# Input projection of a hybrid encoder block: channel groups as one 512-column and one 256-column matmul per weight tile, with the two half sums added after the group

## The chip, the cores and the metric

The kernel runs on one NeuronCore of one Trainium2 chip. The metric is the device time of one execution in microseconds (us); the kernel before takes 1093.23 us, the median of 3 runs (1092.92 to 1093.92). TensorE does the matmuls (PE in the profile, with its weight loads as PEld), VectorE is DVE, ScalarE is ACT, GpSimd is POOL, and SP issues the transfers.

## The reference, cut to what matters

One encoder layer for 256 tokens of width 2048, in float32:

```
h = rmsnorm(x, norm_mix_g)
z = h @ w_in                                   # 2048 x 5120
a, g, q, k, v = split(z)                       # 1024 columns each
u = causal_dwconv(a * sigmoid(g), 31 taps)     # per channel, along tokens
conv_out = silu(layernorm(u))
attn_out = diff_attention(q, k, v)             # 8 heads, rmsnorm per head
x = x + concat(conv_out, attn_out) @ w_out
gate, up = split(rmsnorm(x) @ w_up)            # 2 x 5632 columns
x = x + (gelu(dwconv3(gate)) * up) @ w_down
out = rmsnorm(x)
```

## The kernel before, in words

**Precision by splitting.** A float32 product is made from three matmuls in the type float32r. Every weight chunk is fetched as `raw` (1 MB a transfer, queue of SP), then ACT casts it to `hi` (L156) and DVE computes `lo = raw - hi` (L157), 128 x 1024 elements at a time; the activations stand in `xT` (tile `actT`) as `[P, KD, 2, T]`, high part at index 0 and low part at index 1. A product is hi·high + hi·low + lo·high. The pool of `raw`, `hi` and `lo` has three buffers of each, so ACT and DVE can be at most three chunks ahead of TensorE; a chunk is 4 of the 16 values of k of a group.

**Two ways to build 256 output channels.** `channel_group` (L200) serves the input projection. For each k (16 of them) and each half n of the 256 channels it issues three 256-column matmuls, L206 (hi·high), L207 (hi·low) and L208 (lo·high), all into one accumulator of 128 x 256. `wide_group` (L177) serves the FFN's up projection (44 groups). It issues one 512-column matmul L185 (hi over high and low, which are neighbours in `xT`) into an accumulator of 128 x 2 x 256, and one 256-column matmul L188 (lo over high) into the second half of it. `halves` (L230) then adds the two half sums: ACT copies the second half to a temporary `half` (L232), DVE adds the first half to it (L233).

**Order of the stage.** The first group of a and g channels (j = 0) is built while the input arrives (L260). From then on TensorE's order is written out by hand: for j = 1 to 3 a group of a channels and one of g channels; v columns of heads 0 to 3 (`v_slab`, L216 to L218); then for j = 0 to 3 a group of q and one of k channels, with the remaining v columns after j = 2 and j = 3; then the output projection. That makes 14 groups by `channel_group`. The order on ACT, DVE and SP is chosen by a scheduler that plays the program through with its own cost estimates and priorities; loads are 200 instructions ahead of their place, attention 300.

**What runs beside it.** After every fourth k, `tick` (L166) emits the next background step: attention pieces of the previous head pair (scores L401 and L404, flips L432, values, norm, store L473) and, at two a tick, taps of the 31-tap convolution (L315 to L331; four of six kinds multiply on ACT, L323, and add on DVE, L324; the others are two instructions on DVE, L328). The taps of one channel pair form a chain through its accumulator `cv`. When all are done, `ln_total` (L535) sums the channels on DVE and `ln_mean` (L540) is the matmul that makes the LayerNorm's mean; it has a fixed place in TensorE's order, behind the first two values of k of the output projection.

**What leaves the accumulators before.** For a and g of j = 1 to 3 one DVE multiplication by `rb1` reads the accumulator (L353, L361). For q one ACT copy (L506). For k one DVE multiplication (L511). Each is 128 x 256. The accumulators' pool has four banks, two for each group.

Of the kernel before, what the change touches and what calls it, by code (L numbers as in the profile page):

```python
# [9 lines left out]
F32 = mybir.dt.float32  # L10
F32R = mybir.dt.float32r
AF = mybir.ActivationFunctionType
ALU = mybir.AluOpType
# [3 lines left out]
P = 128  # L17
# [10 lines left out]
def block_kernel(  # L28
# [15 lines left out]
    nc = tc.nc  # L44
    T, D = dims["T"], dims["D"]
    NT = T // P
    KD = D // P
    CONV_K, CC = dims["conv"]
    NCT = CC // P
    H = NCT  # L50
    FK, DFF = dims["ffn"]
    NF = DFF // P
    GW = 2 * P
# [10 lines left out]
    acc = ctx.enter_context(tc.tile_pool(name="acc", bufs=4, space=PSUM))  # L64
# [66 lines left out]
    RATE_A = 2  # L131
    RATE_V = 2
    RATE_Q = 2
# [10 lines left out]
    def load(w, k0, nk, c0, ncol, ahead=None, raw=None):  # L144
        spans = c0 if isinstance(c0, list) else [(c0, ncol)]
        with prio(AHEAD if ahead is None else ahead):
            if raw is None:
                raw = wpool.tile([P, nk, ncol], F32, name="raw")
            fetch(raw, w.tile(k0, nk, spans))
            parts = []  # L150
            hk = min(nk, HALF // ncol)
            for i in range(0, nk, hk):
                hi = wpool.tile([P, hk, ncol], F32R, name="hi")
                lo = wpool.tile([P, hk, ncol], F32R, name="lo")
                src = raw[:, i : i + hk, :]
                nc.scalar.copy(hi, src)  # L156
                nc.vector.tensor_tensor(lo, src, hi.bitcast(F32), op=ALU.subtract)  # L157
                for j in range(hk):
                    parts.append((k0 + i + j, hi[:, j, :], lo[:, j, :]))
        return parts  # L160
# [13 lines left out]
            credit[0] -= 1  # L174
            conv_ops.pop(0)()

    def wide_group(w, c0, xT):  # L177
        ps = [acc.tile([P, 2, T], F32, name="acc") for _ in range(2)]
        for kc in range(0, KD, 8):
            for k, hi, lo in load(w, kc, 8, c0, GW):  # L180
                for n in range(2):
                    cs = slice(n * P, (n + 1) * P)

                    def big(last):
                        nc.tensor.matmul(ps[n], lhsT=hi[:, cs], rhs=xT[:, k], start=(k == 0), stop=last)  # L185

                    def small_(last):
                        nc.tensor.matmul(  # L188
                            ps[n][:, 1, :], lhsT=lo[:, cs], rhs=xT[:, k, 0, :], start=False, stop=last
                        )  # L190

                    if k < KD - 1:
                        big(False)
                        small_(False)
                    else:
                        small_(False)
                        big(True)
        return ps

    def channel_group(w, c0, xT, n_conv=0, ready=None):  # L200
        ps = [acc.tile([P, T], F32, name="acc") for _ in range(2)]
        for kc in range(0, KD, 8):
            for k, hi, lo in ready[kc : kc + 8] if ready else load(w, kc, 8, c0, GW):
                for n in range(2):
                    cs = slice(n * P, (n + 1) * P)
                    nc.tensor.matmul(ps[n], lhsT=hi[:, cs], rhs=xT[:, k, 0, :], start=(k == 0), stop=False)  # L206
                    nc.tensor.matmul(ps[n], lhsT=hi[:, cs], rhs=xT[:, k, 1, :], start=False, stop=False)  # L207
                    nc.tensor.matmul(ps[n], lhsT=lo[:, cs], rhs=xT[:, k, 0, :], start=False, stop=(k == KD - 1))  # L208
                if k % 4 == 3:
                    tick(n_conv)  # L210
        return ps

# [14 lines left out]
    def token_banks(width=XW):  # L227
        return [acc.tile([P, width], F32, name="acc") for _ in range(NT)]

    def halves(dst, ps, pool):  # L230
        t1 = pool.tile([P, T], F32, name="half")
        nc.scalar.copy(t1, ps[:, 1, :])  # L232
        nc.vector.tensor_tensor(dst, ps[:, 0, :], t1, op=ALU.add)  # L233

    with ph1:
        nc.scalar.activation(const.tile([P, 8], F32, name="touch"), mhalf, AF.Copy)
# [3 lines left out]
        xT = shared.tile([P, KD, 2, T], F32R, name="actT")  # L240
        rstd1 = const.tile([P, NT], F32, name="rstd1")
        ss1 = const.tile([P, NT, D // XW], F32, name="ss1")
        rb1 = p1.tile([P, T], F32, name="rb1")
        stage = p1.tile([P, 2, KD * T], F32, name="mixT")
        xraw = stage[:, 0, :].rearrange("p (k t) -> p k t", k=KD)
        wi = w_in
        first = [acc.tile([P, T], F32, name="acc") for _ in range(4)]
# [17 lines left out]
        early = load(wi, 0, 8, GW, GW)  # L265
        for i in range(D // XW):
            if i == 2:
                early.extend(load(wi, 8, 4, GW, GW))
            cs = slice(i * XW, (i + 1) * XW)
# [73 lines left out]
        ordered = ExitStack()  # L343
        ordered.enter_context(tc.manual_schedule(engines={mybir.EngineType.PE}))
        for j in range(NP):
            pa = first[:2] if j == 0 else channel_group(wi, j * GW, xT, n_conv=RATE_A, ready=early if j == 1 else None)
            an, gn = [], []
            for n in range(2):
                a_ = p2.tile([P, T], F32, name=f"a{n}")
                if j == 0:  # L350
                    with prio(ATT):
                        nc.scalar.copy(a_, pa[n])  # L352
                nc.vector.tensor_tensor(a_, a_ if j == 0 else pa[n], rb1, op=ALU.mult)  # L353
                an.append(a_)
            pg = first[2:] if j == 0 else channel_group(wi, CC + j * GW, xT, n_conv=RATE_A)
            for n in range(2):
                g_ = p2.tile([P, T], F32, name="g_")
                if j == 0:
                    with prio(ATT):
                        nc.vector.tensor_copy(g_, pg[n])  # L360
                nc.vector.tensor_tensor(g_, g_ if j == 0 else pg[n], rb1, op=ALU.mult)  # L361
                gn.append(g_)
            for n in range(2):
                c = 2 * j + n
                g_ = gn[n]
                nc.scalar.activation(g_, g_, AF.Sigmoid)
                nc.vector.tensor_tensor(upad[c][:, PADW:], an[n], g_, op=ALU.mult)  # L367
            for k in range(CONV_K):
                conv_ops.append(lambda j=j, k=k: conv_tap(j, k))
# [129 lines left out]

        pending = None  # L500
        for j in range(H // 2):
            pq = channel_group(wi, 2 * CC + j * GW, xT, n_conv=RATE_Q)
            qT, kT = [], []
            for n in range(2):
                q_ = p2.tile([P, T], F32, name=f"q{n}")
                nc.scalar.copy(q_, pq[n])  # L506
                qT.append(q_)
            pk = channel_group(wi, 2 * CC + H * P + j * GW, xT, n_conv=RATE_Q)
            for n in range(2):
                k_ = p2.tile([P, T], F32, name=f"k{n}")  # L510
                nc.vector.tensor_tensor(k_, pk[n], rb1, op=ALU.mult)  # L511
                kT.append(k_)
            a0, a1, a2, a3, a4, a5 = attention(j, qT, kT)
            if j < H // 2 - 1:
                if j < H // 2 - 2:
                    bg.extend([seq(pending, a0), a1, None, None, a2, a3, a4, None])
                else:
                    bg.extend([seq(pending, a0), a1, None, None, None, None, a2, a3, a4])
                pending = a5
            else:  # L520
                last_attention = (a0, a1, a2, a3, a4, a5)
            if j == H // 2 - 2:
                v_slab(H // 2, H // 4)
                bg.extend([None, None, pending])
# [111 lines left out]
    with ExitStack() as ph2:  # L636
# [10 lines left out]
        for j in range(DFF // GW):  # L647
            pg = wide_group(wu, j * GW, h2T)
            ge = []
            for n in range(2):  # L650
                f = 2 * j + n
                gp = gps[f % 4]
                halves(gp[:, FP:], pg[n], q2)
                nc.vector.tensor_tensor(gp[:, FP:], gp[:, FP:], rb2, op=ALU.mult)
                gc = q2.tile([P, T], F32, name=f"gc{n}")
                nc.vector.tensor_scalar(
                    gc, gp[:, 0:T], col["fw"][:, f : f + 1], col["fb"][:, f : f + 1], op0=ALU.mult, op1=ALU.add
                )
                nc.vector.scalar_tensor_tensor(
                    gc, gp[:, 1 : 1 + T], col["fw"][:, NF + f : NF + f + 1], gc, op0=ALU.mult, op1=ALU.add  # L660
                )
                nc.vector.scalar_tensor_tensor(
                    gc, gp[:, 2 : 2 + T], col["fw"][:, 2 * NF + f : 2 * NF + f + 1], gc, op0=ALU.mult, op1=ALU.add
                )
                nc.scalar.activation(gc, gc, AF.Gelu)
                nc.vector.tensor_tensor(gc, gc, rb2, op=ALU.mult)
                ge.append(gc)
            pu = wide_group(wu, DFF + j * GW, h2T)
            for n in range(2):
                f = 2 * j + n  # L670
                us = q2.tile([P, T], F32, name="us")
                halves(us, pu[n], q2)
                nc.vector.tensor_tensor(us, us, ge[n], op=ALU.mult)
                nc.scalar.copy(fT[:, f, 0, :], us)
                nc.vector.tensor_tensor(fT[:, f, 1, :], us, fT[:, f, 0, :].bitcast(F32), op=ALU.subtract)
# [149 lines left out]
```

## Time and profile before

| what | value |
|---|---|
| time, median of 3 runs | 1093.23 us (1092.92 to 1093.92) |
| profiled execution: its time | 1093.6 us |
| profiled execution: first to last instruction (span) | 1091.8 us |
| mean granted TensorE clock | 0.997 of full speed |
| TensorE busy (matmuls) | 1080.2 us, 99% |
| DVE busy | 764.6 us, 70% |
| ACT busy | 599.1 us, 55% |
| L206, L207, L208 (projection groups) | 448 each, 286, 283 and 283 ns mean |
| L185 and L188 (FFN groups) | 1408 each, 395 and 280 ns mean |

The duration of one matmul is longer than the distance from one matmul's start to the next's, because matmuls are pipelined; what a group costs is read from counts in a stretch of time, not from durations. The span and the time differ by 1.8 us that lie before the first and after the last instruction.

### The profile page before, as it was taken

How to read it: one execution, taken by the hardware profiler on the slowest of the kernel's cores; microseconds unless marked ns; L12 is line 12 of the kernel's file. 1: busy time of each engine (PE TensorE's matmuls, PEld its weight loads, DVE VectorE, ACT ScalarE, POOL GpSimd, SP SyncE). 2: the span in 40 equal slices, each digit the busy share in tenths (PEclk: the TensorE clock that was granted, in tenths of full speed). 3: DMA queues.
4: the chain of work that ended last, by engine and by line, in shares of the span. 5: the costliest groups of instructions: out<-in, count | busy, mean ns of one | idle time of the engine just before them, and what ended most of it. 6: DMA issues, size and time to landing. Idle time of an engine off the chain costs nothing.

```text
span 1091.8 us, 16120 instructions
## 1 busy us (share of the span) xinstructions
PE 1080.2 (99%) x6307; PEld 951.6 (87%) x6307; DVE 764.6 (70%) x1201; ACT 599.1 (55%) x974; POOL 16.3 (1%) x44
## 2 busy tenths in 40 slices
PE   9999999999999999999999999999999999999996
PEld 9999999998888888888888888888888888888885
DVE  6799999998665777776777777776777445454544
ACT  6777788886755544544545454444545334343432
POOL 0000000001000000000000000000000000000000
PEclk9999999999999999999999999999999999999998
DMA  9755544453555555555555555555555655555552
GB/s 334 257 185 170 192 164 157 143 189 119 204 179 193 184 182 183 187 189 193 194 193 185 184 183 186 189 193 193 193 189 177 235 196 194 194 195 193 191 176 103
DMA packets 32845, 205.89 MB, mean 189 GB/s; under 512 B 3713, under 2 KB 4481, under 8 KB 9601
## 3 DMA queue, kind: packets, MB, share of 16 engines
q1 hardware_dynamic: 32624, 203.82, 54.0%
q8 instruction: 49, 0.80, 0.3%
q0 software_dynamic: 144, 1.05, 0.2%
q14 instruction: 28, 0.22, 0.1%
HBM read 202.75 MB, written 2.10 MB: 188 GB/s over the span
## 4 chain that ended last, share of the span: by engine, by line
PE 97%; ACT 1%; DVE 1%; DMA 0%; POOL 0%; issue 0%; SPq 0%; POOLq 0%; DVEq 0%; ACTq 0%
PE acc L185 30%; PE acc L188 15%; PE acc L216 11%; PE acc L217 11%; PE acc L218 11%; PE acc L206 5%; PE acc L208 5%; PE acc L207 5%; PE acc L260 2%; PE misc L609 0%; PE misc L404 0%; PE misc L401 0%; DMA v_sb<-in_w_in 0%; PE misc L473 0%; PE misc L432 0%; ACT misc L273 0%
## 5 line engine op out<-in xcount | busy, mean ns | idle before, releaser
L157 DVE TENSOR_TENSOR lo<-raw,hi 128x1024 fp32r<-128x1024 f32 x368 | 449.9, 1223 | 268.9 <-ACT hi L156 268.1
L156 ACT CAST hi<-raw 128x1024 fp32r<-128x1024 f32 x368 | 386.7, 1051 | 392.5 <-PE acc L218 172.7
L185 PE MATMUL acc<-actT,hi 128*128 128x512 f32 x1408 | 481.7, 395 | 0.0
L188 PE MATMUL acc<-actT,lo 128*128 128x256 f32 x1408 | 368.8, 280 | 0.0
L185 PEld LDWEIGHTS acc<-actT,hi 128*128 128x128 f32 x1408 | 253.3, 188 | 48.5
L188 PEld LDWEIGHTS acc<-actT,lo 128*128 128x128 f32 x1408 | 265.4, 188 | 13.7
L217 PE MATMUL acc<-lo,fT 128*128 128x512 f32 (+1 forms) x355 | 137.5, 387 | 0.0
L218 PE MATMUL acc<-hi,fT 128*128 128x512 f32 (+1 forms) x355 | 137.5, 387 | 0.0
L206 PE MATMUL acc<-actT,hi 128*128 128x256 f32 x448 | 128.0, 286 | 0.5 <-ACT a L352 0.5
L208 PE MATMUL acc<-actT,lo 128*128 128x256 f32 x448 | 127.0, 283 | 0.2 <-DVE lo L157 0.2
L207 PE MATMUL acc<-actT,hi 128*128 128x256 f32 x448 | 126.8, 283 | 0.0
L216 PE MATMUL acc<-hi,fT 128*128 128x512 f32 (+1 forms) x355 | 123.8, 387 | 0.0
L206 PEld LDWEIGHTS acc<-actT,hi 128*128 128x128 f32 x448 | 85.9, 192 | 2.0 <-issue 1.0
L208 PEld LDWEIGHTS acc<-actT,lo 128*128 128x128 f32 x448 | 85.9, 192 | 0.4 <-DVE lo L157 0.4
L207 PEld LDWEIGHTS acc<-actT,hi 128*128 128x128 f32 x448 | 85.9, 192 | 0.0
L218 PEld LDWEIGHTS acc<-hi,fT 128*128 128x128 f32 x355 | 66.7, 188 | 13.7
L217 PEld LDWEIGHTS acc<-lo,fT 128*128 128x128 f32 x355 | 66.7, 188 | 13.6
L216 PEld LDWEIGHTS acc<-hi,fT 128*128 128x128 f32 x355 | 66.7, 188 | 13.5
L323 ACT ACTIVATE tap<-u,cols 128x256 f32<-128x256 f32 x160 | 70.7, 503 | 2.7 <-DVE u L367 1.3
L232 ACT COPY half<-acc 128x256 f32<-128x256 f32 x88 | 32.4, 368 | 57.2 <-PE acc L185 57.2
L324 DVE TENSOR_TENSOR cv<-cv,tap 128x512 f32<-128x512 f32 x80 | 54.5, 685 | 1.7
L217 PE MATMUL acc<-lo,mixT 128*128 128x512 f32 x128 | 50.2, 392 | 0.0
(179 smaller groups left out, 914.2 us busy)
## 6 DMA issues: line engine op xcount, KB each, us to landing
raw<-in_w_up SPq DMA_DIRECT2D x88, 1024.0 KB, 4.9
raw<-in_w_down SPq DMA_DIRECT2D x43, 1024.0 KB, 5.0
raw<-in_w_in SPq DMA_DIRECT2D x35, 1024.0 KB, 4.9
raw<-in_w_out SPq DMA_DIRECT2D x14, 1024.0 KB, 4.9
mixT<-in_w_in SPq DMA_DIRECT2D x4, 512.0 KB, 8.6
x_sb<-in_x SPq DMA_DIRECT2D x4, 512.0 KB, 11.1
raw<-in_w_out SPq DMA_DIRECT2D x4, 512.0 KB, 3.5
out<-x_sb SPq DMA_DIRECT2D x8, 256.0 KB, 2.9
```

The source lines that it names most:

```text
L156: nc.scalar.copy(hi, src)
L157: nc.vector.tensor_tensor(lo, src, hi.bitcast(F32), op=ALU.subtract)
L185: nc.tensor.matmul(ps[n], lhsT=hi[:, cs], rhs=xT[:, k], start=(k == 0), stop=last)
L188: nc.tensor.matmul(ps[n][:, 1, :], lhsT=lo[:, cs], rhs=xT[:, k, 0, :], start=False, stop=last)
L206: nc.tensor.matmul(ps[n], lhsT=hi[:, cs], rhs=xT[:, k, 0, :], start=(k == 0), stop=False)
L207: nc.tensor.matmul(ps[n], lhsT=hi[:, cs], rhs=xT[:, k, 1, :], start=False, stop=False)
L208: nc.tensor.matmul(ps[n], lhsT=lo[:, cs], rhs=xT[:, k, 0, :], start=False, stop=(k == KD - 1))
L216: nc.tensor.matmul(ps, lhsT=xT[:, k, 0, ts_], rhs=hi, start=(k == first), stop=False)
L217: nc.tensor.matmul(ps, lhsT=xT[:, k, 0, ts_], rhs=lo, start=False, stop=False)
L218: nc.tensor.matmul(ps, lhsT=xT[:, k, 1, ts_], rhs=hi, start=False, stop=(k == last))
L323: nc.scalar.activation(tmp[:, n, :], upad[c][:, k : k + T], AF.Copy, scale=cwcol(k, c))
L324: nc.vector.tensor_tensor(cv[j], cv[j], tmp, op=ALU.add)
```

## The change: what it does

`channel_group` goes; the 14 groups call `wide_group`, which now takes early loaded chunks and calls `tick` as `channel_group` did. Where the results leave the accumulators, `halves` adds the half sums into the destination, and the multiplication by `rb1` (a, g, k) follows on the sum. `halves` has no temporary: ACT copies the second half to the destination, and DVE adds the first half to it in place; this holds for the FFN's two calls too.

```
-    def wide_group(w, c0, xT):
+    def wide_group(w, c0, xT, n_conv=None, ready=None):
         ps = [acc.tile([P, 2, T], F32, name="acc") for _ in range(2)]
         for kc in range(0, KD, 8):
-            for k, hi, lo in load(w, kc, 8, c0, GW):
+            for k, hi, lo in ready[kc : kc + 8] if ready else load(w, kc, 8, c0, GW):
...
-        return ps
-
-    def channel_group(w, c0, xT, n_conv=0, ready=None):
-        ps = [acc.tile([P, T], F32, name="acc") for _ in range(2)]
...
-                    nc.tensor.matmul(ps[n], lhsT=hi[:, cs], rhs=xT[:, k, 0, :], start=(k == 0), stop=False)
-                    nc.tensor.matmul(ps[n], lhsT=hi[:, cs], rhs=xT[:, k, 1, :], start=False, stop=False)
-                    nc.tensor.matmul(ps[n], lhsT=lo[:, cs], rhs=xT[:, k, 0, :], start=False, stop=(k == KD - 1))
-                if k % 4 == 3:
+                if n_conv is not None and k % 4 == 3:
                     tick(n_conv)
...
-    def halves(dst, ps, pool):
-        t1 = pool.tile([P, T], F32, name="half")
-        nc.scalar.copy(t1, ps[:, 1, :])
-        nc.vector.tensor_tensor(dst, ps[:, 0, :], t1, op=ALU.add)
+    def halves(dst, ps):
+        nc.scalar.copy(dst, ps[:, 1, :])
+        nc.vector.tensor_tensor(dst, ps[:, 0, :], dst, op=ALU.add)
...
-                nc.vector.tensor_tensor(a_, a_ if j == 0 else pa[n], rb1, op=ALU.mult)
+                else:
+                    halves(a_, pa[n])
+                nc.vector.tensor_tensor(a_, a_, rb1, op=ALU.mult)
...
-                nc.vector.tensor_tensor(g_, g_ if j == 0 else pg[n], rb1, op=ALU.mult)
+                else:
+                    halves(g_, pg[n])
+                nc.vector.tensor_tensor(g_, g_, rb1, op=ALU.mult)
...
-                nc.scalar.copy(q_, pq[n])
+                halves(q_, pq[n])
...
-                nc.vector.tensor_tensor(k_, pk[n], rb1, op=ALU.mult)
+                halves(k_, pk[n])
+                nc.vector.tensor_tensor(k_, k_, rb1, op=ALU.mult)
...
-                halves(gp[:, FP:], pg[n], q2)
+                halves(gp[:, FP:], pg[n])
...
-                halves(us, pu[n], q2)
+                halves(us, pu[n])
```

## Rows read from the trace of the kernel before

**Rows 1.** The page: busy time of two engines, and the chain that ended last.

```profile
PE 1080.2 (99%) x6307; PEld 951.6 (87%) x6307; DVE 764.6 (70%) x1201; ACT 599.1 (55%) x974; POOL 16.3 (1%) x44
...
PE 97%; ACT 1%; DVE 1%; DMA 0%; POOL 0%; issue 0%; SPq 0%; POOLq 0%; DVEq 0%; ACTq 0%
```

**Rows 2.** Windows by line: L206 first, L185 second (window, length, busy and count).

```profile
54.00:100.00 46.00, 36.19 (x128) 24.50 (x129) 1.00 0.55 189
...
370.00:840.00 470.00, 459.47 (x1345) 241.62 (x1344) 1.00 0.55 188
```

**Rows 3.** Timeline of PE in a projection group and in an FFN group (start, length).

```profile
54.03 0.28 PE L206 MATMUL acc<-actT,hi 128*128 128x256 f32 x1
54.15 0.28 PE L207 MATMUL acc<-actT,hi 128*128 128x256 f32 x1
...
399.90 0.40 PE L185 MATMUL acc<-actT,hi 128*128 128x512 f32 x1
400.13 0.28 PE L188 MATMUL acc<-actT,lo 128*128 128x256 f32 x1
400.25 0.39 PE L185 MATMUL acc<-actT,hi 128*128 128x512 f32 x1
```

**Rows 4.** Windows: length, then busy PE, PEld, DVE, ACT, POOL; clock, DMA share, GB/s.

```profile
42.60:256.00 213.40, 213.16 (x1683) 204.93 (x1682) 199.20 (x378) 170.04 (x361) 5.66 (x9) 1.00 0.49 166
42.60:101.50 58.90, 58.66 (x489) 58.45 (x488) 54.74 (x88) 41.71 (x73) 0.00 (x0) 1.00 0.52 179
...
123.70:241.00 117.30, 117.30 (x976) 114.14 (x975) 109.64 (x219) 101.60 (x238) 5.66 (x9) 1.00 0.48 162
241.00:256.00 15.00, 15.00 (x122) 13.90 (x121) 13.99 (x40) 10.43 (x25) 0.00 (x0) 1.00 0.33 109
...
349.00:843.00 494.00, 494.00 (x2831) 431.57 (x2830) 360.65 (x577) 245.42 (x357) 1.09 (x6) 1.00 0.54 188
```

**Rows 5.** Waits between 42.6 and 256 us: who waited for whom, total us, times, longest.

```profile
ACT hi L156 <- PE acc L207: 24.8, 29, 1.9
DVE lo L157 <- ACT hi L156: 9.0, 16, 1.1
ACT hi L156 <- PE acc L218: 7.3, 7, 1.7
...
DVE k L511 <- PE acc L208: 1.7, 2, 0.9
```

**Rows 6.** Lines by form over the span (busy, mean ns, idle before), and the tile half's waits.

```profile
L232 ACT COPY half<-acc 128x256 f32<-128x256 f32 x88 | 32.4, 368 | 57.2 <-PE acc L185 57.2
...
L233 DVE TENSOR_TENSOR gp<-acc,half 128x256 f32<-128x256 f32 x44 | 18.5, 421 | 13.7 <-ACT half L232 13.7
...
  ACT half L232: 19.3, 44
```

**Rows 7.** Timeline of DVE after one FFN gate group.

```profile
407.18 0.42 DVE L233 TENSOR_TENSOR gp<-acc,half 128x256 f32<-128x256 f32 x1 [0.63 <-ACT half L232]
407.64 0.42 DVE L654 TENSOR_TENSOR gp<-gp,rb 128x256 f32<-128x256 f32 x1
...
409.57 0.41 DVE L233 TENSOR_TENSOR gp<-acc,half 128x256 f32<-128x256 f32 x1
409.90 0.47 DVE L659 SCALAR_TENSOR_TENSOR gc<-gp,cols,gc 128x256 f32<-128x256 f32 x1
```

**Rows 8.** Timeline of DVE, then of PE, around the end of the convolution.

```profile
247.98 0.68 DVE L324 TENSOR_TENSOR cv<-cv,tap 128x512 f32<-128x512 f32 x1
...
253.41 1.22 DVE L157 TENSOR_TENSOR lo<-raw,hi 128x1024 fp32r<-128x1024 f32 x1 [1.01 <-ACT hi L156]
...
255.62 0.40 DVE L535 TENSOR_TENSOR part<-part,cv 128x256 f32<-128x256 f32 x1
...
257.71 0.59 PE L540 MATMUL misc<-part,onesc 128*128 128x256 f32 x2
```

More of the change, by code (lines that the diff above doesn't have):

```diff
@@ L197, in wide_group @@
                         big(True)
-        return ps
-    def channel_group(w, c0, xT, n_conv=0, ready=None):
-        ps = [acc.tile([P, T], F32, name="acc") for _ in range(2)]
[L202 to L205, printed above, removed]
-                    nc.tensor.matmul(ps[n], lhsT=hi[:, cs], rhs=xT[:, k, 0, :], start=(k == 0), stop=False)
-                    nc.tensor.matmul(ps[n], lhsT=hi[:, cs], rhs=xT[:, k, 1, :], start=False, stop=False)
-                    nc.tensor.matmul(ps[n], lhsT=lo[:, cs], rhs=xT[:, k, 0, :], start=False, stop=(k == KD - 1))
-                if k % 4 == 3:
+                if n_conv is not None and k % 4 == 3:
                     tick(n_conv)
@@ L345, in block_kernel @@
         for j in range(NP):
-            pa = first[:2] if j == 0 else channel_group(wi, j * GW, xT, n_conv=RATE_A, ready=early if j == 1 else None)
+            pa = first[:2] if j == 0 else wide_group(wi, j * GW, xT, n_conv=RATE_A, ready=early if j == 1 else None)
             an, gn = [], []
@@ L352, in block_kernel @@
                         nc.scalar.copy(a_, pa[n])
-                nc.vector.tensor_tensor(a_, a_ if j == 0 else pa[n], rb1, op=ALU.mult)
+                else:
+                    halves(a_, pa[n])
+                nc.vector.tensor_tensor(a_, a_, rb1, op=ALU.mult)
                 an.append(a_)
-            pg = first[2:] if j == 0 else channel_group(wi, CC + j * GW, xT, n_conv=RATE_A)
+            pg = first[2:] if j == 0 else wide_group(wi, CC + j * GW, xT, n_conv=RATE_A)
             for n in range(2):
@@ L501, in block_kernel @@
         for j in range(H // 2):
-            pq = channel_group(wi, 2 * CC + j * GW, xT, n_conv=RATE_Q)
+            pq = wide_group(wi, 2 * CC + j * GW, xT, n_conv=RATE_Q)
             qT, kT = [], []
@@ L505, in block_kernel @@
                 q_ = p2.tile([P, T], F32, name=f"q{n}")
-                nc.scalar.copy(q_, pq[n])
+                halves(q_, pq[n])
                 qT.append(q_)
-            pk = channel_group(wi, 2 * CC + H * P + j * GW, xT, n_conv=RATE_Q)
+            pk = wide_group(wi, 2 * CC + H * P + j * GW, xT, n_conv=RATE_Q)
             for n in range(2):
                 k_ = p2.tile([P, T], F32, name=f"k{n}")
-                nc.vector.tensor_tensor(k_, pk[n], rb1, op=ALU.mult)
+                halves(k_, pk[n])
+                nc.vector.tensor_tensor(k_, k_, rb1, op=ALU.mult)
                 kT.append(k_)
```

## The prediction

> **What bounds the kernel now.** I read the page first. TensorE is busy for 99% of the span and has 97% of the chain that ended last, so a change pays only if TensorE's own stream gets shorter, and costs only if something makes TensorE wait [rows 1]. The average says nothing about who is next, so I then cut the span into stages. In the FFN stage DVE is busy for 360.65 of 494 us, 73%. In the stage that is changed, from 42.6 us (when `rb1` is there) to 256 us (when the convolution's sum is done), it is busy for 199.2 of 213.4 us, 93%, and in the part from 42.6 to 101.5 us also 93%; ACT has 170.0 of 213.4, 80% [rows 4]. So the same construction that has room in the FFN meets an engine with 14.2 us of idle time here.
>
> The waits say of what kind these 14.2 us are. DVE waited 9.0 us for `hi`, and ACT's casts to `hi` waited 24.8 and 7.3 us for TensorE to release a buffer [rows 5]. That is back pressure: conversions run as far ahead as three buffers allow. Those 9.0 us can be filled with work before TensorE notices. The other 5.2 us are small gaps, among them 1.7 us in which a k multiplication stood at the head of DVE's queue until its group ended [rows 5].
>
> **TensorE's part.** The change removes 14 x 16 x 2 = 448 triples of 256-column matmuls and puts a 512-column and a 256-column matmul in the place of each. In the projection 128 triples pass in 46.00 us, 0.359 us each; in the FFN 1345 pairs pass in 470.00 us, 0.349 us each [rows 2]. The starts agree: 0.12 us from one 256-column matmul to the next, against 0.23 us behind a 512-column one and 0.12 behind its partner [rows 3]. The gain is 448 x 0.010 = 4.5 us. The upper bound is the same, since the FFN's pair is this very instruction pair on the same layout; the lower bound is nothing, if here a 512-column matmul took two steps of 0.12 us.
>
> The Trainium skill gives another price (TensorE: Matmul & The Clock Gate, Wait — 56ns, not 53.3ns?): a warm matmul starts N / 2.4 GHz plus about 2.5 ns after the one before, so that joining two 256-column matmuls into one saves only that 2.5 ns. An estimate by the Trainium skill is 448 x 2.5 ns = 1.1 us instead of 4.5. The rows disagree with it in this stream, where each matmul comes with a weight load of its own: 120 ns at 256 columns, where the Trainium skill's formula gives 109 [rows 3].
>
> The granted clock is 1.00 before and in the FFN stage alike, the level of 2.4 GHz [rows 4], and no pause is added that is longer than those the stage has, so I count nothing for it. The number of transfers and their order by group stay; 4.5 us less over the stage is about 2% more GB/s, and the FFN stage takes 188 GB/s at that pace against 166 here [rows 4]. If that cover were gone, the next thing late would be `raw`.
>
> **What DVE and ACT get.** Each of 28 results (12 of a and g, 8 of q, 8 of k) has one DVE addition more, and 20 have an ACT copy that they did not have; q's copy existed. The multiplications stay, reading SBUF instead of the accumulator. An ACT copy takes 368 ns [rows 6], so ACT gets 20 x 0.37 = 7.4 us more; it has 43.4 us idle in the stage [rows 4], so I count nothing. If ACT were full, `hi` and the convolution's products would be late next.
>
> An addition takes 421 ns [rows 6], but what it occupies is the distance to the next start: 0.33 us when an unrelated instruction follows, 0.46 us when the multiplication of its own result follows [rows 7]. So 28 additions cost DVE between 9.2 and 12.9 us; I take the middle, 11.1, since with two results in flight both orders occur. They may also wait for their ACT copy. In the FFN such waits are 19.3 us for 88 additions, 0.22 us each [rows 6], which would be 6.1 us here; behind them on DVE would stand the next `lo` and the taps, and TensorE would wait for those. I take nothing for this wait, because a DVE that runs late finds the copy done. Both ends stay in the range.
>
> **Where it is felt.** DVE's order can put `lo` first and the convolution's taps behind, but the taps have a deadline: `ln_total` must be done before L540, which has a fixed place on TensorE. The last tap starts at 247.98, the last `ln_total` addition at 255.62 and ends at 256.02, and L540 starts at 257.71 without a wait [rows 8]. All 14 groups lie before it, so with TensorE's gain L540 comes up at 253.2. DVE then has 253.2 - 42.6 = 210.6 us for 199.2 of old work [rows 4], less 1.2 for the `lo` at 253.41 that can go behind [rows 8], plus 11.1 of additions: 209.1 us. With the 5.2 us of small gaps it needs 214.3. TensorE waits 3.7 us at L540, or earlier for a `lo` or for a k that DVE brings late.
>
> The bounds of this stall: nothing, if additions cost 0.33 each and the gaps close too (207.2 of work in 210.6); and 199.2 + 12.9 + 5.2 + 6.1 - 210.6 = 12.8 us, if all is dear and nothing can go behind. After L540 nothing is regained, since the rest of the chain is TensorE's.
>
> **What costs nothing.** `halves` without a temporary: the same two instructions with another address; the buffers of `us` and `gp` were last read a group earlier, and TensorE does not wait in the FFN. The accumulators: the same four banks; a bank must be free one group, some 11 us, after its group ended, and copy, addition and multiplication take about 1.2 us. The results of k: scores come 24 old matmuls, now 8 pairs or 2.8 us, after the group; copy and two DVE steps are about 1.2 us, so some 1.6 us are left for queueing. If that is gone, the scores L401 are the place where TensorE waits; this is the same stall as above at another place, and is not counted twice.
>
> **Sum.** The profiled execution took 1093.6 us: 1093.6 - 4.5 + 3.7 = 1092.8. The median is 0.4 lower than that execution, so 1092.4.
>
> **The rivals.** First, *the gain stays whole*: DVE's extra work fills only idle time. For it: 9.0 us of idle are back pressure, ACT's casts wait for TensorE 32 us in the stage, and the taps can be drawn from anywhere in a long list. Against it: 210.6 us for 209.1 of work leaves 1.5 us, with no gap. It gives 1093.2 - 4.5 = 1088.7. All of this case with a stall under 2.3 us: chance 0.33.
>
> Second, on the other side, *DVE becomes the bound*: additions wait at the head of DVE's strict order for their ACT copies, and the debt falls due at L540. Each addition dear (0.46) and with the FFN's wait (0.22) makes the stall of 12.8 us: 1093.2 + 8.3 = 1101.5. It decides from a stall of 6.7 us on, that is, when the additions cost 0.11 us each more than in my sum. For it: DVE 93% and ACT 87% busy between 123.7 and 241 us (101.6 of 117.3 [rows 4]), with taps that go to and fro between both. Against it: half the spare time is real back pressure. Chance 0.25.
>
> Third, *no gain from the width*: 512 columns cost 0.24 us here, TensorE saves nothing, but L540 then comes 4.5 us later and the stall of 3.7 is covered: 1093.2. Rows 2 and 3 speak against it; chance 0.05.
>
> My forecast, a stall of 2.3 to 6.7 us, has 0.37.
>
> **How the numbers follow.** What a measurement of this kernel can tell is about 0.2%, 2.2 us. Faster is the first rival, 0.33; the same are the forecast and the third, 0.42; slower is the second, 0.25. The forecast's own range is 1091.0 to 1095.4. The range for 8 in 10 goes to the whole gain, 1088.5, and into the second rival up to a stall of 9.3 us, 1098.0.
>
> **What would show it.** On TensorE: 448 pairs at 0.349 us, the FFN's starts of 0.23 and 0.12, in place of 0.12 three times. On DVE between 42.6 us and L535: busy 208 to 212 us and nearly no wait for `hi`. On ACT: fewer waits for TensorE's release. At L540, L401 or a `lo` matmul: TensorE's idle time of some 4 us that before had none; the FFN, the output projection and the tail with their old lengths. It would be wrong in sign if DVE's static order left it waiting for copies while taps were ready, and wrong in size if the scheduler, which plays the new program through, moves taps into the time before 42.6 us or lets scores wait for k in each of the four rounds.

## The result, and the profile after

The kernel with the change takes 1100.05 us (median of 6 runs, 1098.96 to 1100.22) against 1093.07 us for the kernel before (6 runs, 1092.79 to 1093.92). The ratio is 1.0058, with a 95% interval of 1.0048 to 1.0069: slower by 7.0 us, above the range of 1088.5 to 1098.0 us and in the second rival's case, DVE as the bound. The profiled execution took 1100.12 us with a span of 1098.3, 6.5 more than the span before.

The page of the kernel after, its busy times and its chain, beside [rows 1]:

```profile
PE 1077.4 (98%) x5859; PEld 927.0 (84%) x5859; DVE 773.9 (70%) x1229; ACT 605.3 (55%) x994; POOL 15.9 (1%) x44
...
PE 93%; DVE 3%; ACT 2%; DMA 1%; issue 0%; SPq 0%; POOL 0%; POOLq 0%; DVEq 0%; ACTq 0%
```

The 448 matmuls fewer and the 28 DVE instructions more are there (6307 to 5859, 1201 to 1229). TensorE's share of the chain fell from 97% to 93%, and what it lost went mostly to DVE (1% to 3%) and ACT (1% to 2%): somewhere TensorE waits for them. Over the whole execution the waits of TensorE (waiting line and what it waited for; total us, times, longest) say where:

```profile
PE misc L533 <- DVE part L528: 6.0, 1, 6.0
...
PE misc L393 <- DVE k L504: 1.5, 1, 1.5
...
PE misc L465 <- ACT osb L455: 0.4, 1, 0.4
PE acc L188 <- DVE lo L157: 0.3, 1, 0.3
```

L533 is the mean matmul, which was L540 in the kernel before and did not wait there [rows 8]; L528 is `ln_total`. The scores' first matmul (L393) waits for a k.

TensorE itself did become faster. One timeline of PE in a projection group (start, length) and the window of the L185 matmuls alone, the answers to [rows 3] and [rows 2]:

```profile
53.65 0.39 PE L185 MATMUL acc<-actT,hi 128*128 128x512 f32 x1
53.88 0.28 PE L188 MATMUL acc<-actT,lo 128*128 128x256 f32 x1
54.00 0.39 PE L185 MATMUL acc<-actT,hi 128*128 128x512 f32 x1
```

```profile
54.00:100.00 46.00, 45.62 (x131) 24.16 (x131) 1.00 0.53 186
```

131 pairs in 46.00 us are 0.351 us each, against 0.359 for a triple.

Where the time went is read from the starts of the same instruction in both timelines of PE:

| TensorE's place | before, us | after, us | difference |
|---|---|---|---|
| first q group | 123.70 | 122.02 | -1.7 |
| scores of j = 1 | 177.69 | 174.91 | -2.8 |
| scores of j = 3 | 244.31 | 243.15 | -1.2 |
| output projection's first matmul | 254.96 | 253.79 | -1.2 |
| mean matmul | 257.71 | 262.93 | +5.2 |
| FFN's first matmul | 349.65 | 356.16 | +6.5 |
| end of the span | 1091.8 | 1098.3 | +6.5 |

So there are three pieces. TensorE gains up to 2.8 us on the way and gives 1.6 of it back before the output projection, 1.5 of that in the wait for k. It then loses 6.4 us up to the mean matmul, nearly all in the one wait of 6.0 us. And from the mean matmul to the FFN it loses 1.3 us more (91.94 us before, 93.24 after). From the FFN on nothing changes.

The windows of the kernel after answer to [rows 4] (length, then busy PE, PEld, DVE, ACT, POOL; clock, DMA share, GB/s):

```profile
42.20:262.60 220.40, 212.48 (x1270) 183.29 (x1268) 211.34 (x410) 177.57 (x383) 6.34 (x9) 1.00 0.47 163
...
238.20:253.80 15.60, 14.09 (x118) 13.09 (x116) 15.45 (x41) 13.24 (x36) 0.00 (x0) 1.00 0.31 102
...
262.90:267.20 4.30, 4.28 (x13) 3.60 (x14) 2.61 (x8) 2.67 (x6) 0.00 (x0) 0.50 0.33 120
267.20:270.00 2.80, 2.80 (x18) 2.40 (x17) 2.50 (x5) 1.66 (x3) 0.00 (x0) 0.97 0.00 0
```

The first row is the stage up to the end of the convolution's sum: DVE has 211.3 us of work in it and 9.1 us without (the sum's second addition ends at 262.87, 0.27 us behind this window, all of it work). In the last stretch before the output projection (second row) DVE is busy for 15.45 of 15.60 us. The third row follows straight on the wait of 6.0 us: the granted clock is 0.50, the 1.2 GHz level, for 4.3 us, and then comes back. What that costs is read from the same matmul of the output projection, the seventh behind the mean matmul and the transposes that follow it, in the kernel before and then in the kernel after:

```profile
260.17 0.39 PE L216 MATMUL acc<-hi,mixT 128*128 128x512 f32 x1
```

```profile
267.61 0.40 PE L205 MATMUL acc<-hi,mixT 128*128 128x512 f32 x1
```

It starts 2.46 us after the mean matmul before (257.71) and 4.68 us after it now (262.93): the low clock costs 2.2 us. Up to the FFN 0.9 us of it come back, 0.8 at the small matmuls of attention and LayerNorm that stand next between two of the output projection, which took 1.88 us before (268.11 to 269.99) and take 1.04 us now (275.56 to 276.60). What is left is the 1.3 us.

DVE's own queue shows what was late. Its timeline in the kernel after around the end of the convolution, and that of PE, beside [rows 8]:

```profile
254.76 1.20 DVE L157 TENSOR_TENSOR lo<-raw,hi 128x1024 fp32r<-128x1024 f32 x1
...
257.40 1.22 DVE L157 TENSOR_TENSOR lo<-raw,hi 128x1024 fp32r<-128x1024 f32 x1
258.54 0.68 DVE L312 TENSOR_TENSOR cv<-cv,tap 128x512 f32<-128x512 f32 x1
259.14 0.74 DVE L415 SCALAR_TENSOR_TENSOR pr<-pr,sm 128x128 f32<-128x128 f32 x2
259.80 0.68 DVE L327 TENSOR_TENSOR tap<-tap,cv 128x512 f32<-128x512 f32 x1
260.40 1.22 DVE L157 TENSOR_TENSOR lo<-raw,hi 128x1024 fp32r<-128x1024 f32 x1
...
261.99 0.88 DVE L528 TENSOR_TENSOR part<-part,cv 128x256 f32<-128x256 f32 x2
```

```profile
256.56 0.39 PE L207 MATMUL acc<-hi,mixT 128*128 128x512 f32 x1
262.93 0.80 PE L533 MATMUL misc<-part,onesc 128*128 128x256 f32 x1 [5.98 <-DVE part L528]
```

The last tap starts at 258.54, 10.6 us later than before (247.98), and three `lo` (254.76, 257.40, 260.40) stand ahead of `ln_total` though TensorE reads them only behind the mean matmul (the first two values of k of the output projection read the `lo` before these, from 252.88). DVE has no idle time to speak of here (it is busy for 8.73 of the 8.80 us from 253.8 to 262.6): it is late with work.

### The profile page after: what moved, and what is told of

The parts are those of the page before. It is cut to its first block, busy times and chain, and to the rows that moved or that the text cites. A ratio compares the mean times of both kernels' runs of the same rounds, so it can differ in the third digit from the quotient of the medians.

```text
span 1098.3 us, 15280 instructions
## 1 busy us (share of the span) xinstructions
PE 1077.4 (98%) x5859; PEld 927.0 (84%) x5859; DVE 773.9 (70%) x1229; ACT 605.3 (55%) x994; POOL 15.9 (1%) x44
## 4 chain that ended last, share of the span: by engine, by line
PE 93%; DVE 3%; ACT 2%; DMA 1%; issue 0%; SPq 0%; POOL 0%; POOLq 0%; DVEq 0%; ACTq 0%
PE acc L185 39%; PE acc L188 19%; PE acc L205 11%; PE acc L206 11%; PE acc L207 11%; PE acc L248 1%; DVE lo L157 1%; DMA v_sb<-in_w_in 1%; ACT tap L311 1%; ACT hi L156 0%; DVE cv L312 0%; SPq L139 0%; PE misc L602 0%; PE misc L424 0%; ACT osb L446 0%
## 5 line engine op out<-in xcount | busy, mean ns | idle before, releaser
L185 PE MATMUL acc<-actT,hi 128*128 128x512 f32 x1856 | 640.7, 396 | 0.5 <-ACT a L340 0.5
L185 PEld LDWEIGHTS acc<-actT,hi 128*128 128x128 f32 x1856 | 336.8, 188 | 69.1 <-issue 1.3
L206 PE MATMUL acc<-lo,fT 128*128 128x512 f32 (+1 forms) x355 | 137.5, 387 | 0.0
L206 PEld LDWEIGHTS acc<-lo,fT 128*128 128x128 f32 x355 | 66.7, 188 | 13.5
L206 PE MATMUL acc<-lo,mixT 128*128 128x512 f32 x128 | 50.8, 396 | 0.0
L207 PE MATMUL acc<-hi,mixT 128*128 128x512 f32 x128 | 50.2, 392 | 0.0
L205 PE MATMUL acc<-hi,mixT 128*128 128x512 f32 x128 | 49.1, 398 | 0.0
L316 DVE SCALAR_TENSOR_TENSOR cv<-u,cols,cv 128x256 f32<-128x256 f32 x80 | 34.9, 477 | 0.2
L220 ACT COPY gp<-acc 128x256 f32<-128x256 f32 x44 | 16.2, 368 | 32.6 <-PE acc L185 32.6
L205 PE MATMUL acc<-hi,actT 128*128 128x256 f32 (+1 forms) x96 | 31.0, 323 | 0.0
L206 PE MATMUL acc<-lo,actT 128*128 128x256 f32 (+1 forms) x96 | 30.5, 318 | 0.0
L207 PE MATMUL acc<-hi,actT 128*128 128x256 f32 (+1 forms) x96 | 30.5, 318 | 0.0
## 6 DMA issues: line engine op xcount, KB each, us to landing
x_sb<-in_x SPq DMA_DIRECT2D x4, 512.0 KB, 11.1
out<-x_sb SPq DMA_DIRECT2D x8, 256.0 KB, 2.8
```

The lines of the kernel that those rows point to most:

```text
L205: nc.tensor.matmul(ps, lhsT=xT[:, k, 0, ts_], rhs=hi, start=(k == first), stop=False)
L206: nc.tensor.matmul(ps, lhsT=xT[:, k, 0, ts_], rhs=lo, start=False, stop=False)
L207: nc.tensor.matmul(ps, lhsT=xT[:, k, 1, ts_], rhs=hi, start=False, stop=(k == last))
L220: nc.scalar.copy(dst, ps[:, 1, :])
L316: nc.vector.scalar_tensor_tensor(cv[j][:, n, :], upad[c][:, k : k + T], cwcol(k, c), cv[j][:, n, :], op0=ALU.mult, op1=ALU.add,)
```

## The experiments

Two explanations were tried: the additions' time on DVE falls due at the mean matmul, with no room left to hide it (theory 1), or DVE's order, made for shorter groups, is what makes the sum late (theory 2). Each kernel was timed in several rounds against the kernel before on the same chip; ratios come with 95% intervals. Lines are those of each kernel.

**The additions left out (e1_no_add).** The second half sum is not added, so the output lacks that part; matmuls stay paired, and the 28 additions and 20 copies are gone.

```diff
-                    halves(a_, pa[n])
-                nc.vector.tensor_tensor(a_, a_, rb1, op=ALU.mult)
+                nc.vector.tensor_tensor(a_, a_ if j == 0 else pa[n][:, 0, :], rb1, op=ALU.mult)
...
-                halves(q_, pq[n])
+                nc.scalar.copy(q_, pq[n][:, 0, :])
```

> The pairs of matmuls stay, but the 28 results of the projection are read from the first half sum alone: no ACT copy and no DVE addition for them, so the hi.low and lo.high products are left out of a, g, q and k. Theory 1 (the additions fill DVE, so that the convolution's sum comes late and TensorE waits for it at the mean matmul): no wait there, and TensorE's whole gain of 4.5 us shows, 1088.6 us, 1087.5 to 1090. Theory 2 (the order: a group is now 64 matmuls long and not 96, so that loads, which are placed 200 instructions ahead, overtake more taps, with or without additions): the wait at the mean matmul stays at 3 to 6 us and the time at 1096 to 1100.

It took 1093.57 us, ratio 1.0003 [0.9993, 1.0012]: neither theory's time. TensorE reaches the output projection 3.8 us sooner after its stage's start than in the kernel before (250.61 against 254.96, with DVE's first `lo` behind `rb1` at 42.63 against 43.19), so the gain is real. But then it waits, which theory 1 had excluded and theory 2 had said. The wait at the mean matmul, DVE's timeline there, and the windows of this kernel:

```profile
PE misc L532 <- DVE part L527: 3.4, 1, 3.4
```

```profile
254.21 0.42 DVE L527 TENSOR_TENSOR part<-part,cv 128x256 f32<-128x256 f32 x1
254.69 1.23 DVE L157 TENSOR_TENSOR lo<-raw,hi 128x1024 fp32r<-128x1024 f32 x1
255.84 0.74 DVE L415 SCALAR_TENSOR_TENSOR pr<-pr,sm 128x128 f32<-128x128 f32 x2
256.49 0.42 DVE L527 TENSOR_TENSOR part<-part,cv 128x256 f32<-128x256 f32 x1
```

```profile
42.20:256.95 214.75, 210.98 (x1269) 182.94 (x1268) 202.39 (x382) 171.70 (x363) 5.28 (x9) 1.00 0.48 167
257.00:261.00 4.00, 4.00 (x13) 3.33 (x14) 2.37 (x8) 2.42 (x6) 0.00 (x0) 0.50 0.34 123
```

Without one addition the sum ends at 256.9, against 256.0 before. DVE is idle for 12.4 us of this stage (214.75 - 202.39), though TensorE waits for it in the end: idle time early in the stage is not used to be ready sooner at its end. Two `lo` more than before also stand ahead of the sum's end (72 against 70, some 2.4 us), one of them between the two additions of `ln_total`. So in this order TensorE alone does not move the mean matmul; what would come through with these two `lo` behind the sum, no run shows. Beside the kernel after, e1 prices the additions: with them the time is 6.0 us longer (1.0058 against 1.0003), and the sum ends 6.0 us later (262.87 against 256.91). The clock falls to 0.50 behind this wait of 3.4 us too.

**The additions alone (e5_adds_on_before).** The kernel before with its 256-column triples; a, g, q and k get copy and addition as in the change, so they come out doubled. (A first form, e2_adds_alone, with the triples spread over both halves of a wider accumulator, gave no result.)

```diff
+    def twice(dst, ps):
+        nc.scalar.copy(dst, ps)
+        nc.vector.tensor_tensor(dst, ps, dst, op=ALU.add)
...
-                nc.scalar.copy(q_, pq[n])
+                twice(q_, pq[n])
...
-                nc.vector.tensor_tensor(k_, pk[n], rb1, op=ALU.mult)
+                twice(k_, pk[n])
+                nc.vector.tensor_tensor(k_, k_, rb1, op=ALU.mult)
```

> The kernel before, its three 256-column matmuls and its single accumulator kept, with 20 ACT copies and 28 DVE additions put behind the groups as in the change (the accumulator is added to its own copy, so a, g, q and k are doubled): the additions without the pairs. Theory 1 (DVE debt: additions before the mean matmul make it late): DVE has 28 x 0.33 = 9.3 us more to do, of which idle time takes some 3 to 5, so the mean matmul waits some 4 to 6 us and the clock falls behind it: 1097 to 1100. Theory 2 (order: shorter groups let loads overtake the taps): groups are 96 matmuls long as before, 1093 to 1095.

1101.15 us, 1.0066 [1.0051, 1.0082]: the additions alone cost 7.7 us, with the old matmuls, somewhat more than theory 1 had said. The waits of TensorE in this kernel:

```profile
PE misc L549 <- DVE part L544: 2.5, 1, 2.5
...
PE misc L409 <- DVE k L520: 1.9, 1, 1.9
```

The mean matmul starts at 264.54, against 262.93 with the pairs. Its wait is short only because TensorE comes late itself: the granted clock is 0.50 behind the wait for k (252.0 to 254.6), and the output projection starts at 259.12, against 254.96 before. The groups are 96 matmuls long as before, and the sum still ends 8.5 us later (264.48 against 256.02). So the additions alone make it late, as theory 1 says, and shorter groups are not needed for it.

**Less other work for DVE (e6_after_27_taps, e7_before_27_taps, g3_no_add_27).** The convolution has 27 taps in place of 31: in the kernel after, in the kernel before, and in the kernel after without the additions. The output lacks these taps.

```diff
-            for k in range(CONV_K):
+            for k in range(CONV_K - 4):
                 conv_ops.append(lambda j=j, k=k: conv_tap(j, k))
```

> The changed kernel with 27 of the convolution's 31 taps (k = 27 to 30 left out for every channel), which takes 4 x (3 x 0.60 + 0.79) = 10.4 us of work from DVE ahead of the mean matmul, about what the additions put there, and 12 x 0.8 = 9.8 us from ACT. Theory 1: the wait of 6.0 us and the clock's fall behind it go, and TensorE's gain of 4.5 us shows: 1088 to 1091. Theory 2, or a gain that never was: 1094 or more.

> The control: the kernel before with the same 27 taps. Theory 1: TensorE's own stream is its limit, 1092.5 to 1093.5, so that the difference to the changed kernel with 27 taps is the pairs' gain alone, 3 to 4.5 us. If the kernel before is itself held by DVE somewhere, it falls too, to 1090 or less.

> Pairs without the additions (second half sums left out of a, g, q and k) and with 27 taps: TensorE's gain with nothing in its way. In the run without additions the projection stage up to the output projection's first matmul was 4.1 us shorter and the wait of 3.4 us at the mean matmul took it back. Theory 1: that wait goes and the whole 4.1 us show, 1088.5 to 1089.5. If something else holds the stage: 1091 or more.

1090.40 (0.9969 [0.9957, 0.9980]), 1092.99 (0.9998 [0.9989, 1.0008]) and 1089.19 us (0.9963 [0.9950, 0.9977]). The kernel before gains nothing from fewer taps, the kernel after 9.7 us (1100.05 to 1090.40), and the wait at the mean matmul is gone. With room on DVE the change as it stands is worth 2.6 us (1092.99 - 1090.40), and the pairs without additions 3.8 (1092.99 - 1089.19; 1092.99 and 1089.19 come from different chips, and by the ratios the difference is 0.35%, again 3.8). One reservation: four taps less are 10.4 us of DVE's work, but in these kernels the sum ends at 237.8, 229.2 and 226.4, 19 to 27 us ahead of the mean matmul. Taps are emitted two a tick, so 16 fewer also end up to eight ticks sooner in the order. The runs show what the pairs are worth with the sum out of TensorE's way, and not how much of that is work and how much is place.

**Where work stands in the order (e8_after_ahead, e4_mean_later, h1_lo_behind).** Three edits meant to change the order alone, with the whole computation: less head start for the loads' chain; sum and mean matmul one tick later; and two `lo` held back behind `ln_total`.

```diff
-    AHEAD = -200
+    AHEAD = -135
```

```diff
-        bg.extend([seq(ln_total, ln_mean, a2, a3), a4, None, seq(a5, ln_var), ln_apply])
+        bg.extend([seq(a2, a3), seq(ln_total, ln_mean, a4), None, seq(a5, ln_var), ln_apply])
```

```diff
+                sub = nc.vector.tensor_tensor(lo, src, hi.bitcast(F32), op=ALU.subtract)
+                if behind and behind[1] > 0:
+                    after(sub, behind[0])
+                    behind[1] -= 1
...
+                last = nc.vector.tensor_tensor(ln["part"], ln["part"], cv[NP - 1][:, n, :], op=ALU.add)
+            behind.extend([last, 2])
```

> The changed kernel with loads 135 instead of 200 instructions ahead, the same stretch of a group as before the change (135/64 against 200/96). Theory 2: the taps come back to their places and most of the loss goes: 1093 to 1096. Theory 1: the work on DVE is the same, 1099 to 1101.

> The changed kernel with the sum and the mean matmul one place later in TensorE's order, that is behind 12 more matmuls of 0.227 us. Both theories: TensorE does 2.7 us of work before it waits, so the wait falls from 6.0 to about 3.3 us: 1096 to 1098; with a shorter wait the clock may not fall, which would be some 1.3 us more, 1095. If later steps of the LayerNorm then make TensorE wait, the time stays near 1099.

> The changed kernel with two of the lo computations that DVE did ahead of the convolution's sum, though TensorE uses them behind the mean matmul, put behind the sum: 2 x 1.14 = 2.3 us less ahead of it, with the same work in all. If the place of lo in DVE's order is that part of the debt: the wait of 6.0 us falls to 3.7, and 1100 to 1097.5, 1096.5 to 1098.5; the clock falls behind this wait as behind the 3.4 us of the run without additions. If the sum waits for something else than DVE's turn (the taps' own chain): 1099.5 to 1100.5.

e8 took 1099.16 us (1.0054 [1.0039, 1.0069]) with the same 6.0 us at the mean matmul. But its edit moved nothing: in its trace every engine's instructions, and the transfers, stand in the order of the kernel after. It repeats that kernel, and whether the head start has a part in the loss stays untested. e4 took 1101.72 (1.0071 [1.0056, 1.0086]), more than was expected: the wait at the mean matmul is gone, and waits of 2.3 us each for DVE stand at two later places of TensorE, beside the old 1.5 for k, with the granted clock down behind both (0.56 from 263 to 265 us, 0.50 from 275 to 280). A debt put off is still paid. h1 took 1098.13 (1.0040 [1.0027, 1.0054]). DVE's and PE's timeline of h1:

```profile
259.95 0.89 DVE L532 TENSOR_TENSOR part<-part,cv 128x256 f32<-128x256 f32 x2
260.75 2.35 DVE L158 TENSOR_TENSOR lo<-raw,hi 128x1024 fp32r<-128x1024 f32 x2
```

```profile
260.89 1.22 PE L538 MATMUL misc<-part,onesc 128*128 128x256 f32 x2 [3.83 <-DVE part L532]
```

Two `lo` behind the sum take 2.2 us off the wait (6.0 to 3.8) and 1.9 off the time, while the work is the same. So about a third of the wait is place in DVE's order. That is theory 2's kind of cause, but shorter groups do not explain it: ahead of the sum's end stand 70 `lo` in the kernel before, 72 in the kernel after and in e1, but also 71 in e5, where all groups have their old length, and 72 in h2 (below), where ten of 14 have it. Why the scheduler puts them there, no run settles.

**Work taken off DVE (e3_pool_ag, g2_act_taps, g1_pool_taps).** GpSimd does the 12 multiplications of a and g by `rb1`; ACT does the products of one tap in six more; GpSimd sums five taps of each pair apart, 16 additions.

```diff
-                nc.vector.tensor_tensor(a_, a_, rb1, op=ALU.mult)
+                (nc.vector if j == 0 else nc.gpsimd).tensor_tensor(a_, a_, rb1, op=ALU.mult)
...
-    ACT_TAPS = (0, 1, 3, 4)
+    ACT_TAPS = (0, 1, 2, 3, 4)
...
+            if k in POOL_TAPS:
...
+                    nc.gpsimd.tensor_tensor(cvp[j], cvp[j], tmp, op=ALU.add)
```

> The changed kernel with the 12 multiplications by rb1 of a and g (j = 1 to 3) on GpSimd in place of DVE. Theory 1: 12 x 0.33 = 4.0 us less on DVE before the mean matmul, so the wait of 6.0 us falls to about 2 and the clock does not fall behind it: 1094 to 1096. Theory 2: no change, 1099 to 1101.

> The changed kernel with five instead of four of six taps multiplied on ACT: 20 taps change, DVE has 20 x 0.19 = 3.8 us less and ACT 20 x 0.8 = 16 us more in a stage in which ACT was idle for 43 us. Theory 1: the wait at the mean matmul falls from 6.0 to some 2 to 3 us, 1095 to 1098. If ACT is the next bound, the k copies and casts are late: 1100 or more.

> The changed kernel, its whole computation, with 16 of the convolution's additions moved from DVE to GpSimd: for five taps of each channel pair ACT's products are summed in an accumulator of their own, and DVE adds it once. DVE has 20 x 0.60 - 4 x 0.60 = 9.6 us less to do ahead of the mean matmul, as much as the 28 additions of half sums put there. Theory 1 (DVE debt): the wait of 6.0 us at the mean matmul goes and TensorE's gain shows, as with 27 taps: 1089.5 to 1092. If products held for GpSimd (some 3 to 5 us for an addition of 128x512) stop ACT's next products, or GpSimd slows DVE: 1094 or more.

e3 took 1096.63 us (1.0032 [1.0020, 1.0043]): no wait at the mean matmul, but TensorE waits 3.8 us for k and 1.8 for `lo`. g2 took 1098.28 (1.0045 [1.0031, 1.0059]), with 5.4 us at the mean matmul where 2 to 3 were expected: DVE's work ahead of the sum's end fell by 3.5 us (211.6 to 208.1), but its idle time grew by 2.3 (9.1 to 11.3), so the stage got only 1.2 us shorter. g1, meant to take the most off, was the worst: 1101.36 (1.0072 [1.0060, 1.0085]), with 3.5 us for k, 2.5 for `osb` (an attention result that TensorE transposes) and 2.2 for `lo`. Groups by line and shape in g1 (busy us, mean ns), DVE first and then GpSimd:

```profile
L325 DVE TENSOR_TENSOR cv<-cv,tap 128x512 f32<-128x512 f32 x60 | 46.8, 783 | 0.7
L329 DVE SCALAR_TENSOR_TENSOR cv<-u,cols,cv 128x256 f32<-128x256 f32 x80 | 39.9, 536 | 0.3
L517 DVE TENSOR_TENSOR k<-k,rb 128x256 f32<-128x256 f32 x8 | 4.1, 508 | 0.0
```

```profile
L310 POOL TENSOR_TENSOR v_sb<-v_sb,tap 128x512 f32<-128x512 f32 x16 | 30.0, 1878 | 143.3 <-ACT tap L308 143.3
```

The same groups in the kernel after:

```profile
L312 DVE TENSOR_TENSOR cv<-cv,tap 128x512 f32<-128x512 f32 x80 | 54.7, 684 | 2.0 <-ACT tap L311 0.6
L316 DVE SCALAR_TENSOR_TENSOR cv<-u,cols,cv 128x256 f32<-128x256 f32 x80 | 34.9, 477 | 0.2
...
L504 DVE TENSOR_TENSOR k<-k,rb 128x256 f32<-128x256 f32 x8 | 3.3, 414 | 0.0
```

The taps' additions that stayed on DVE grew from 684 to 783 ns, the fused taps from 477 to 536 and k's multiplications from 414 to 508. In the first two groups alone that is 60 x 0.099 + 80 x 0.059 = 10.7 us, more than the 16 additions of some 0.60 us (the step from a tap's addition to the next start, 258.54 to 259.14 above) that DVE no longer had. The growth lies in the instructions that ran beside an addition of GpSimd: ten of the 60 additions of taps took 1293 ns on average, the other 50 took 681. Two such cases, on DVE and then on GpSimd:

```profile
136.95 1.45 DVE L325 TENSOR_TENSOR cv<-cv,tap 128x512 f32<-128x512 f32 x1
149.84 1.15 DVE L517 TENSOR_TENSOR k<-k,rb 128x256 f32<-128x256 f32 x1
```

```profile
136.11 1.75 POOL L310 TENSOR_TENSOR v_sb<-v_sb,tap 128x512 f32<-128x512 f32 x1 [7.72 <-ACT tap L308]
148.48 2.22 POOL L310 TENSOR_TENSOR v_sb<-v_sb,tap 128x512 f32<-128x512 f32 x1 [10.62 <-ACT tap L308]
```

The sum is not late in g1 (it ends at 240.2, 26 us ahead of the mean matmul). TensorE waits for DVE at other places instead, first of all for the k of the second case, and the granted clock is 0.52 from 150.8 to 154.3 us behind that wait and 0.51 from 185.0 to 188.5.

**Pairs in the q groups alone (h2_q_only).** 4 of the 14 groups have pairs and half sums, 8 additions.

```diff
-                    halves(a_, pa[n])
-                nc.vector.tensor_tensor(a_, a_, rb1, op=ALU.mult)
+                nc.vector.tensor_tensor(a_, a_ if j == 0 else pa[n], rb1, op=ALU.mult)
...
-            pk = wide_group(wi, 2 * CC + H * P + j * GW, xT, n_conv=RATE_Q)
+            pk = channel_group(wi, 2 * CC + H * P + j * GW, xT, n_conv=RATE_Q)
```

> Pairs and half sums for the four q groups alone (they had an ACT copy before, so only 8 DVE additions come in), everything else as before. TensorE gains 128 x 0.009 = 1.2 us, DVE gets 8 x 0.33 = 2.7 us ahead of a sum that was ready 1.7 us before the mean matmul. By DVE's debt the gain is paid back: 1093 to 1096. If DVE's idle time takes the additions: 1091.5 to 1092.5.

1097.97 us, 1.0040 [1.0027, 1.0052], worse than expected: 8 additions, 8 x 0.33 = 2.6 us of DVE's time, cost 4.4, with a wait of 4.2 us at the mean matmul. A stretch of this kernel up to the sum's end:

```profile
42.60:260.00 217.40, 213.21 (x1558) 198.40 (x1556) 203.99 (x389) 172.32 (x362) 6.22 (x9) 1.00 0.47 165
```

DVE is idle for 13.4 us of it (217.40 - 203.99), 7.7 of them in 14 waits for `hi`, about what it had before; and three `lo` again stand ahead of the sum between 252.06 and 258.93, so that 72 stand ahead of its end and not 70, another 2.4 us. So the idle time stayed idle, and the additions and two `lo` came on top. Why so little of it was filled here and more in the kernel after, no run settles.

## Why the prediction was wrong

**Right.** TensorE's gain: 4.5 us predicted, 3.8 with the sum out of the way (g3 against e7), and 3.8 up to the output projection in e1. The Trainium skill's price for it (TensorE: Matmul & The Clock Gate, Wait — 56ns, not 53.3ns?), 1.1 us by estimate, does not agree with these runs. Also right: the place where the bill comes, the mean matmul behind `ln_total`; that additions hardly wait for their copies (0.8 us in the stage); that a late k is the next thing to make TensorE wait; that ACT has room, and that accumulators, temporaries and the FFN cost nothing.

**Mis-sized, with little effect: the additions.** 11.1 us predicted, from 0.33 to 0.46 us each. DVE's busy time grew by 9.3 us (764.6 to 773.9), 0.33 each: the cheap end.

**The step that failed: "Where it is felt".** It gave DVE 214.3 us up to the end of the sum, and TensorE a stall of 3.7. DVE took 220.7 (42.2, where `rb1` is there in this kernel, to 262.87), 6.4 more, of which 2.5 are work (211.6 against 209.1) and 3.9 idle time (9.1 against 5.2).

The work: I let one `lo` go behind the sum. In the trace 72 `lo` stand in the stage against 70 before, where I had counted 69, so three more at some 1.2 us each; the cheaper additions take 1.8 back, which leaves about 1.8 of the 2.5. These `lo` of the output projection stand in DVE's fixed order ahead of taps that are due first. h1 shows what this alone is worth: 1.9 us for two `lo`.

The idle time: "Those 9.0 us can be filled with work before TensorE notices" was the wrong assumption. The waits of the kernel after in the stage, beside [rows 5]:

```profile
ACT hi L156 <- PE acc L185: 14.8, 20, 1.8
...
ACT hi L156 <- PE acc L207: 4.6, 5, 1.7
DVE lo L157 <- ACT hi L156: 4.3, 10, 0.8
```

DVE's wait for `hi` shrank from 9.0 to 4.3 us, not to nothing, and the small gaps stayed (4.8 us, against 5.2): of 14.2 us of idle time 5.1 were filled. DVE takes its queue in order, and while a `lo` stands at its head waiting for `hi`, what is behind it doesn't run. The kernel before has such a case, beside [rows 8]:

```profile
251.81 0.40 DVE L341 TENSOR_TENSOR part<-tap 128x256 f32<-128x256 f32 x1
...
254.56 0.42 DVE L535 TENSOR_TENSOR part<-part,cv 128x256 f32<-128x256 f32 x1
```

The first addition of `ln_total` reads the `part` that is there at 252.21, and runs at 254.56, behind the `lo` of 253.41 that waited 1.01 us for its `hi`. That the rest of the idle time was lost in this way too is argued and not shown; e1 and h2 show that it stays, with 12.4 and 13.4 us. The prediction's own sum with the measured sizes, 199.2 + 2.4 for two more `lo` + 9.3 for the additions + 9.1 of idle time, gives 220.0, against 220.7 measured.

**TensorE's side of the stall.** I had L540 come up 4.5 us sooner. It would have been ready at 256.95 (262.93 - 5.98), 214.7 us after the stage's start against 215.1 before, so only 0.4 sooner: the k's margin of 1.6 us was used up (a wait of 1.5), and some smaller gaps went with it. I had said that such a wait is the same stall at another place; it is, and with it the stall is 6.0 + 1.5 = 7.5 us, over the 6.7 from which the second rival was to decide.

**The clock, counted at nothing.** The argument was that no pause is added; with a pause of 6.0 us it fell. It cost 2.2 us behind the mean matmul, at 0.50 for 4.3 us, of which 0.9 came back before the FFN.

From the median before, 1093.07: -3.8 for the pairs, +2.6 given back on the way in the wait for k (1.5) and smaller gaps (so that -1.2 stand at the output projection), +6.4 up to the mean matmul, +1.3 behind it (2.2 for the clock, less 0.9), together +6.5 as the spans have it; the medians differ by 7.0.

The rival that came true had the right mechanism for another reason. Its price was dear additions and waits for copies; both were cheap. What decided was that DVE's order could use little of its idle time, and that two more `lo` came ahead of the sum. That the kernel before was on that edge already could have been read from [rows 8]: the sum ends 1.7 us ahead of the matmul that reads it, and [rows 4] show DVE busy for 13.99 of the last 15.0 us. A gain of 4.5 us for TensorE could not come through whole unless the sum came sooner too, additions or not; in e1 nothing of it came through.

## What to carry to other kernels

Before counting a faster TensorE, find the next result that another engine owes it and ask how far ahead it is ready: the slack there (1.7 us here) is the most that the gain can be unless that engine gets ready sooner too, however much idle time it shows on average. Idle time of an engine that runs its queue in order is spare only if the instruction at the head of the queue is the one that waits for nothing; here idle time early in the stage did not make the result at its end earlier. Where an edit adds work to such an engine ahead of a due result, count most of the work (the additions' 9.3 us cost 6.0 in the kernel after and 7.7 in e5), and the instructions of the next stage that slip in ahead of the result as well.

## What the hardware showed that I had not expected

TensorE's granted clock fell to 0.50 behind a wait of 6.0 us and one of 3.4 us, and stood there for some 4 us behind it; the kernel before has no pause in this stretch and 1.00 throughout. A stall here costs more than its length: the matmuls behind it took 2.2 us more in the kernel after. The length alone does not tell whether the clock falls: behind a wait of 1.9 us in e5 it was 0.50 (252.0 to 254.6), behind one of 2.7 us in e3 it was 1.00 (247.2 to 252.0).

GpSimd's additions are not free to DVE. While 16 of them, 1.88 us each, ran in g1, DVE's own instructions in the same kernel became 12% to 23% longer on average (the three groups above). All of it lies in those that ran beside one of these additions: the tap's addition of 136.95, begun while GpSimd's addition of 136.11 was under way, took 1.45 us in place of 0.68 and ended 0.54 us after it. An addition of a k's half sum, which has the accumulator as one input, ran beside GpSimd's addition of 148.48 and kept its 0.41 us. The Trainium skill says that a DVE instruction with two inputs in SBUF contends with a GpSimd instruction that reads SBUF, at a port pair that they share and that one of them holds alone (SBUF — State Buffer, Who interferes with whom). The trace agrees: in the cases shown it was DVE that was held back, as a longer instruction and not as a wait.
